# y split where it is made and loaded over h^T; wider weight ring in the RG phase; last block in written order

## The chip, the cores and the metric

One core of a Trainium2 chip runs the whole program. The metric is the device time of one execution in microseconds (us). Beside it stands the profiled execution, whose span runs from its first to its last instruction.

## What is computed

One layer of a hybrid mixer on 1024 latent tokens of width D = 2048, with 256 context tokens whose final states seed the latent scans. Cut to the latent path:

```python
hx = rmsnorm(x, norm_g) * (1 + sc_x) + sh_x           # shift, scale, gate: silu(c) @ w_mod
px = split(hx @ w_in)                                 # q k | v | o | z | gates | xr | zr
h  = mlstm_bidir(conv_silu(q, k), v, gates)           # 4 heads, column-major token order
ym = rmsnorm_per_head(h) * m_norm_g * sigmoid(o) * silu(z)
xl = dwconv(xr)                                       # RG-LRU: 1024 channels
r, i = sigmoid(w_r . xl + b_r), sigmoid(w_i . xl + b_i)   # block-diagonal, both directions
a  = exp(-8 * r * softplus(-lam))
hr = scan(a, sqrt(1 - a**2) * i * xl)                 # forward plus backward
yr = hr * silu(zr)
x  = x + gt_x * (concat([ym, yr]) @ w_out)
return rmsnorm(x, final_g)
```

## The kernel before

Every float32 product is made of three TensorE (PE) products of fp32r halves: a tile t is split into t_hi = fp32r(t), a copy on ScalarE (ACT), and t_lo = t - t_hi, a subtraction on VectorE (DVE), and hi.hi, hi.lo and lo.hi are summed in PSUM.

**h^T and y.** The normed input stands transposed in SBUF as 16 pairs hxh[j], hxl[j] of 128x1024. The output projection needs y in the same form, and y tile j takes the place of hxh[j], hxl[j], once the last unit that reads h^T is past it. A y tile is 128 channels x 1024 tokens. Two come from each of four heads, eight from the RG blocks (RG0 to RG7, 128 channels each). Fifteen go to a DRAM tensor yD, one DMA each on ACT's queue (L981 for the RG blocks, a like line at the end of each head); the last, RG7's, is split straight into hxh[15], hxl[15] (L978, L979).

**Weights.** Class Ring streams w_in and w_out: SyncE (SP) loads raws of 128x1024 (512 KB) into two buffers, each raw is cut into pieces of 128x512, split by ACT (whi, L228) and DVE (wlo, L229), in order, three pieces ahead at most. In the output phase three more pieces are added (ring.widen). A unit's 96 matmuls of w_in read four pieces (ct_unit, L1276, L1279, L1282), a block of the output 16 pieces, one for each j.

**The RG phase.** For each i there is a unit xr and a unit zr (sigmoid and product at L1459 and near it), and a generator x_rg that runs beside the units: convolution (POOL L740, three DVE steps L742), the split of the result xs/xl (ACT L1388, DVE L1389), eight gate tiles of three matmuls each (L1394 to L1396) into PSUM, sigmoids (ACT L935), the products i*x (POOL L937), exp and tanh (ACT L948, L949), sqrt (L952), then on DVE a sum and two products (L957, L958), the scan (L959), for both directions; POOL adds the two (L969), DVE multiplies by the gate (L973).

**The y stage.** From the last zr unit (zr7) on, y tiles are loaded in halves of 128x512 on GpSimd's (POOL) queue into two buffers (y_load, yst, L1422), and split over h^T by ACT (L1438) and DVE (L1439), 30 times: the half with tokens 0 to 511 ahead of out(0,0), two tiles for a hook at each j; the other half within the blocks that follow.

**The output phase.** out_unit(hf, db) makes 512 tokens x 512 columns: 16 j x 4 token tiles x 3 matmuls (L1475 to L1477) into one PSUM tile mm of two halves and two tiles mx. A hook of the next block evacuates it: times gt (DVE L1512), plus x from a tile xpc (POOL or DVE, L1513; one buffer), Square with its sum into fst (ACT L1514, which writes its square back to the PSUM tile), times final_g (L1515). After the fourth block of a token half, finish() takes the mean, square root and reciprocal (L1519 to L1521) and scales and stores (L1524 to L1527). The last block (1,3) has its weights in the place of y tiles of h^T, and goes token tile by token tile (L1563 to L1565).

**Order.** Units and generators are interleaved by a clock that the program runs when it is built; the instructions of each engine then stand in a fixed order that a list scheduler sets from priorities, and an engine works in that order. A DMA queue is the sequence of DMA starts on its engine; up to eight of POOL's are under way at a time.

Of the kernel before, what the change touches and what calls it, by code (L numbers as in the profile page):

```python
# [257 lines left out]
def tile_hymba(ctx: ExitStack, tc: tile.TileContext, x, x_t, ctx_t, vecs_t, w_mod_a, w_mod_g, b_mod, w_in,  # L258
# [21 lines left out]
    yD = dram.tile([16, 128, SEQ], F32, name="yD")  # L280
# [1135 lines left out]
    def y_load(hf, pool, bufs):

        done, ts = ysp[hf]
        while len(ts) < bufs and done + len(ts) < KT - 1 and ("y", KORD[done + len(ts)]) in xflag:
            j = done + len(ts)  # L1420
            t = pool.tile([128, 512], F32, tag="gw", bufs=bufs, name=f"yst{hf}_{j}")
            POOL.dma_start(out=t, in_=yD[KORD[j]][:, 512 * hf:512 * hf + 512])  # L1422
            ts.append(t)

    def y_split(n, hf, pool, bufs):

        for _ in range(n):
            j, ts = ysp[hf]
            if j >= KT - 1:
                clk.until(lambda: ("y", KORD[j]) in xflag)  # L1430
                return
            if not ts:
                clk.until(lambda: ("y", KORD[j]) in xflag)
                y_load(hf, pool, bufs)
            t = ts.pop(0)
            o = slice(512 * hf, 512 * hf + 512)
            with hp(tc, P['y']):
# [4 lines left out]

    for n, i in enumerate(RG_ORDER[1:]):
# [86 lines left out]
    for hf in range(2):  # L1530
        for db in range(4):
            if (hf, db) != (0, 0):
                todo = pend

                def hook(j):
                    if todo and j == 0:
                        vecs(*todo[0:2])
# [8 lines left out]
                    if hf and db == 0 and j == 0:
                        y_split(KT, 1, op, GWB)
                    if hf == 0 and db >= YD0 and j % 2 == 0 and j >= YJ0:
                        y_split(1, 1, op, GWB)

# [73 lines left out]
```

## Time and profile before

| | |
|---|---|
| median of three runs | 1891.2 us (1890.71 to 1900.89) |
| the profiled execution | 1890.24 us, span 1888.5 |
| PE busy | 1815.2 us, 96% |
| DVE, ACT, POOL busy | 896.5, 779.7, 284.5 us |
| mean granted PE clock | 0.99 |
| DMA | 224.5 MB, 119 GB/s |

Where PE's row is nearly full, the time is that of its matmuls and what breaks them. Two things break them: a wait for another engine's result, which the list of waits names, and a clock below 1.00 of 2.4 GHz, which stands in the windows. A window's count of matmuls holds both, so it is compared with the count of a stretch in which nothing happens.

### The profile page before, as it was taken

To read this page: it belongs to the slowest core of one execution; us is meant where nothing else is said; L and a number is where in the kernel's file an instruction comes from. 1 tells how busy PE (TensorE), PEld (TensorE's weight loads), DVE (VectorE), ACT (ScalarE), POOL (GpSimd) and SP (SyncE) were. 2 spreads that over 40 slices of the span, in tenths; PEclk is the share of its full clock that TensorE was granted. 3 is DMA by queue.
4 is the path that set the end of the run, shared out by engine and by line. 5 is a ranking of instruction groups with operands and counts; after the bars stand their busy time and mean duration, and the time that the engine had idled before them with its cause. 6 is when DMAs were issued, how large, how long until landed. Compare 5 with 4: busy or idle time off the path is not lost.

```text
span 1888.5 us, 24095 instructions
## 1 busy us (share of the span) xinstructions
PE 1815.2 (96%) x9114; PEld 1483.5 (79%) x9114; DVE 896.5 (47%) x1632; ACT 779.7 (41%) x1209; POOL 284.5 (15%) x382
## 2 busy tenths in 40 slices
PE   6998999999999999999999999999999989999996
PEld 2557999787897879887898877777888767888775
DVE  5576552446424654345425433564444555334422
ACT  5346542356445331233112333655555634233311
POOL 0000000012002200011001201232112323222220
PEclk9999999999999999999999999999999999999998
DMA  9975674223212433333332213112112345446523
GB/s 381 398 248 158 174 194 108 58 54 76 78 47 58 105 109 107 88 93 81 92 111 81 55 46 106 51 58 58 46 50 59 128 144 179 137 141 221 168 92 117
DMA packets 225365, 224.50 MB, mean 119 GB/s; under 512 B 25664, under 2 KB 184528, under 8 KB 225248
## 3 DMA queue, kind: packets, MB, share of 16 engines
q1 hardware_dynamic: 217200, 199.17, 35.1%
q10 hardware_dynamic: 5264, 14.88, 2.1%
q0 software_dynamic: 2784, 8.92, 1.4%
q8 instruction: 71, 1.16, 0.3%
q14 instruction: 46, 0.38, 0.1%
HBM read 202.92 MB, written 20.00 MB: 118 GB/s over the span
## 4 chain that ended last, share of the span: by engine, by line
PE 61%; DMA 12%; issue 11%; DVE 7%; ACT 6%; POOL 3%; SPq 0%; ACTq 0%; POOLq 0%; DVEq 0%
PE mm L1282 11%; PE mm L1276 11%; PE mm L1279 11%; DMA xpc<-in_x_dram 5%; PE mm L1319 2%; PE mm L1321 2%; PE mm L1322 2%; DMA yst<-yD 2%; POOL res L1513 2%; PE mm L627 2%; PE mx L505 1%; DMA r<-in_w_mod_g_dram 1%; PE mx L1207 1%; DMA wm<-in_w_mod_a_dram 1%; PE mx L1208 1%
## 5 line engine op out<-in xcount | busy, mean ns | idle before, releaser
L229 DVE TENSOR_TENSOR wlo<-raw,whi 128x512 fp32r<-128x512 f32 (+2 forms) x396 | 288.0, 736 | 574.5 <-ACT whi L228 568.3
L228 ACT ACTIVATE whi<-raw 128x512 fp32r<-128x512 f32 (+2 forms) x396 | 243.2, 624 | 561.5 <-PE mm L1279 247.2
L1276 PE MATMUL mm<-hxh,whi 128*128 128x512 f32 x1184 | 385.5, 406 | 0.3 <-DVE Gx L1308 0.3
L1282 PE MATMUL mm<-hxh,wlo 128*128 128x512 f32 x1184 | 375.1, 398 | 4.2 <-DVE wlo L229 4.2
L1279 PE MATMUL mm<-hxl,whi 128*128 128x512 f32 x1184 | 372.0, 395 | 0.0
L1282 PEld LDWEIGHTS mm<-hxh,wlo 128*128 128x128 f32 x1184 | 223.0, 189 | 57.9 <-DVE wlo L229 6.7
L1279 PEld LDWEIGHTS mm<-hxl,whi 128*128 128x128 f32 x1184 | 222.9, 188 | 52.9
L1276 PEld LDWEIGHTS mm<-hxh,whi 128*128 128x128 f32 x1184 | 221.5, 189 | 49.6 <-ACT s L1306 0.5
L1319 PE MATMUL mm<-whi,hxh 128*128 128x256 f32 x384 | 110.2, 287 | 0.3 <-DVE s L1357 0.2
L1321 PE MATMUL mm<-wlo,hxh 128*128 128x256 f32 x384 | 108.1, 281 | 0.0
L1322 PE MATMUL mm<-whi,hxl 128*128 128x256 f32 x384 | 107.4, 281 | 0.0
L1475 PE MATMUL mm<-whi,hxh 128*128 128x512 f32 x224 | 90.1, 402 | 6.3 <-ACT whi L228 6.1
L1476 PE MATMUL mm<-wlo,hxh 128*128 128x512 f32 x224 | 90.4, 404 | 3.3 <-DVE wlo L229 3.3
L1477 PE MATMUL mm<-whi,hxl 128*128 128x512 f32 x224 | 89.4, 399 | 0.0
L1476 PE MATMUL mx<-wlo,hxh 128*128 128x512 f32 x224 | 89.0, 397 | 0.0
L1475 PE MATMUL mx<-whi,hxh 128*128 128x512 f32 x224 | 89.0, 400 | 0.0
L1477 PE MATMUL mx<-whi,hxl 128*128 128x512 f32 x224 | 88.8, 396 | 0.0
L1033 DVE SCALAR_TENSOR_TENSOR r<-r,cols,r 128x256 f32<-128x256 f32 x120 | 60.5, 504 | 38.0 <-DMA r<-in_w_mod_g_dram 35.9
L1319 PEld LDWEIGHTS mm<-whi,hxh 128*128 128x128 f32 x384 | 72.4, 189 | 1.1 <-PE mx L1256 0.6
L1321 PEld LDWEIGHTS mm<-wlo,hxh 128*128 128x128 f32 x384 | 72.4, 188 | 0.3
L1322 PEld LDWEIGHTS mm<-whi,hxl 128*128 128x128 f32 x384 | 72.2, 189 | 0.0
L1179 ACT ACTIVATE D<-D,gxAC 128x128 f32<-128x128 f32 x64 | 25.5, 401 | 112.8 <-POOL D L1178 112.7
(324 smaller groups left out, 3086.5 us busy)
## 6 DMA issues: line engine op xcount, KB each, us to landing
raw<-in_w_in_dram SPq DMA_DIRECT2D x134, 512.0 KB
wm<-in_w_mod_a_dram SPq DMA_DIRECT2D x64, 512.0 KB
raw<-in_w_out_dram SPq DMA_DIRECT2D x64, 512.0 KB
r<-in_w_mod_g_dram SPq DMA_DIRECT2D x128, 128.0 KB
xT<-in_x_t_dram SPq DMA_DIRECT2D x16, 512.0 KB
NI<-niD SPq DMA_DIRECT2D x64, 128.0 KB
xpc<-in_x_dram SPq DMA_DIRECT2D x32, 256.0 KB
yD<-s ACTq DMA_DIRECT2D x15, 512.0 KB
```

What stands on the lines that cost most here:

```text
L228: self.nc.scalar.activation(out=hi, in_=src, func=AF.Copy)
L229: self.nc.vector.tensor_tensor(out=lo, in0=src, in1=hi.bitcast(F32), op=SUB)
L1033: DVE.scalar_tensor_tensor(out=a, in0=t, scalar=silc[:, k:k + 1], in1=a, op0=MUL, op1=ADD)
L1276: PE.matmul(out=ps[:, ts], lhsT=hi, rhs=hxh[k][:, ts], start=(k == 0), stop=False)
L1279: PE.matmul(out=ps[:, ts], lhsT=hi, rhs=hxl[k][:, ts], start=False, stop=False)
L1282: PE.matmul(out=ps[:, ts], lhsT=lo, rhs=hxh[k][:, ts], start=False, stop=(k == KT - 1))
L1319: PE.matmul(out=o, lhsT=hxh[k][:, sl], rhs=hi, start=(k == 0 and tt % 2 == 0), stop=False, skip_group_check=True)
L1321: PE.matmul(out=o, lhsT=hxh[k][:, sl], rhs=lo, start=False, stop=False, skip_group_check=True)
L1322: PE.matmul(out=o, lhsT=hxl[k][:, sl], rhs=hi, start=False, stop=(k == KT - 1), skip_group_check=True)
L1475: PE.matmul(out=pst[jt], lhsT=hxh[j][:, sl], rhs=hi, start=(j == 0), stop=False)
L1476: PE.matmul(out=pst[jt], lhsT=hxh[j][:, sl], rhs=lo, start=False, stop=False)
L1477: PE.matmul(out=pst[jt], lhsT=hxl[j][:, sl], rhs=hi, start=False, stop=(j == KT - 1))
```

## The change

- yD becomes two DRAM tensors. put_y splits each of the fifteen y tiles where it is made: an ACT copy of 128x1024 into a free tile (og in a head, the backward scan's tile in an RG block), a DVE subtraction of 128x1024 in place, a store of the hi part on ACT's queue and of the lo part on SP's.
- y_load and y_split go, and with them 30 ACT copies and 30 DVE subtractions of 128x512. y_fill loads hi and lo of a whole tile (128x1024, 512 KB) into hxh[j], hxl[j]: 30 loads, 15.7 MB where 7.9 MB were read, all on POOL's queue, from zr7's step 2 on, as its steps leave the tiles.
- ring.widen adds two pieces (whi and wlo) from the RG phase on; they go at j = 9 of out(0,0), before the output phase's three come.
- xpc has two buffers and is loaded two tiles ahead; the Square writes to an SBUF tile; the sum of three of the four parts of the mean is taken at db = 2, the square root takes the fourth.
- The last block keeps written order on PE, and each of its token tiles has a PSUM tile of its own to begin with: mx, mx, a half of mm, a half of another mm.

The diff, cut to its core:

```diff
-    yD = dram.tile([16, 128, SEQ], F32, name="yD")
+    yD = [dram.tile([16, 128, SEQ], F32, name=f"yD{u}") for u in range(2)]
...
-                ACT.dma_start(out=yD[8 + i], in_=y)
+                put_y(8 + i, y, it[1][:, 0:T])
...
+    def put_y(n, y, w):
+
+        act(out=w.bitcast(F32R), in_=y, func=AF.Copy)
+        DVE.tensor_tensor(out=y.bitcast(F32R), in0=y, in1=w, op=SUB)
+        ACT.dma_start(out=yD[0][n], in_=w)
+        SP.dma_start(out=yD[1][n], in_=y)
...
-            ACT.dma_start(out=yD[2 * h + v], in_=Y[v][:, 0:SEQ])
+            put_y(2 * h + v, Y[v][:, 0:SEQ], og[v][:, 0:SEQ])
+            yield 1.2
...
-            t = pool.tile([128, 512], F32, tag="gw", bufs=bufs, name=f"yst{hf}_{j}")
-            POOL.dma_start(out=t, in_=yD[KORD[j]][:, 512 * hf:512 * hf + 512])
...
-                act(out=hxh[j][:, o], in_=t, func=AF.Copy)
-                DVE.tensor_tensor(out=hxl[j][:, o], in0=t, in1=hxh[j][:, o].bitcast(F32), op=SUB)
...
+    def y_fill(k):
+
+        while y_n[0] <= min(k, KT - 2) and ("y", KORD[y_n[0]]) in xflag:
+            j = y_n[0]
+            POOL.dma_start(out=hxh[j], in_=yD[0][KORD[j]])
+            POOL.dma_start(out=hxl[j], in_=yD[1][KORD[j]])
+            y_n[0] += 1
+
+    def y_wait(j):
+        if j >= 9:
+            ring.x = None
+        clk.until(lambda: ("y", KORD[j]) in xflag)
+        y_fill(KT)
+
+    ring.widen(rg, 0, NXG, 1024, 512)
...
-        ps = ct_unit(("zr", i), (lambda k: y_load(0, rg, YB) if k < K0 else y_split(1, 0, rg, YB) if k < K1 else None) if last else None)
+        ps = ct_unit(("zr", i), (lambda k: y_fill(k - 2)) if last else None)
...
-    pst = out_unit(0, 0, lambda j: y_split(2, 0, rg, YB))
+    pst = out_unit(0, 0, y_wait)
...
-        t = op.tile([128, 512], F32, tag="xpc", bufs=1, name=f"xpc{tt}_{db}")
+        t = op.tile([128, 512], F32, tag="xpc", bufs=2, name=f"xpc{tt}_{db}")
...
-            act(out=ps, in_=r, func=AF.Square, accum_out=fst[tt][:, db:db + 1])
+            jk = op.tile([128, 512], F32, tag="jk", bufs=1, name=f"jk{tt}_{db}")
+            act(out=jk, in_=r, func=AF.Square, accum_out=fst[tt][:, db:db + 1])
...
+            if db == 2:
+                f = fst[tt]
+                DVE.tensor_reduce(out=f[:, 4:5], in_=f[:, 0:3], axis=AX.X, op=ADD)
+                DVE.tensor_scalar(out=f[:, 4:5], in0=f[:, 4:5], scalar1=1.0 / D, scalar2=EPS, op0=MUL, op1=ADD)
...
-        DVE.tensor_reduce(out=f[:, 4:5], in_=f[:, 0:4], axis=AX.X, op=ADD)
-        act(out=f[:, 5:6], in_=f[:, 4:5], func=AF.Sqrt, scale=1.0 / D, bias=eps)
+        act(out=f[:, 5:6], in_=f[:, 3:4], func=AF.Sqrt, scale=1.0 / D, bias=f[:, 4:5])
...
-    pst = out_tiles(3)
-    for jt in range(4):
+    pst = [mx_tile(), mx_tile(), mm_tile()[:, 0:512], None]
+    with in_order(tc, PE.engine):
+        for jt in range(4):
+            if jt == 3:
+                pst[3] = mm_tile()[:, 0:512]
```

Three places show what moved. In the rows a name's number is the buffer's own, `L...` the line of its kernel (most lines of the kernel after are 1 lower), and the words in brackets are the engines or DMA lanes whose results are waited for.

On POOL, at the last RG block: L937 (after: L936) are RG7's two products, L969 (L968) the sum of its scans. Before:

```order
L1422 DMA yst0_7_12427<-yD_72 128x512 [waits DMASW5_49,DVE_49]
L1422 DMA yst0_8_12516<-yD_72 128x512 [waits DMAHW3_49,DMASW6_49,DVE_49]
L1422 DMA yst0_9_12520<-yD_72 128x512 [waits DMASW7_49,DVE_49]
L1422 DMA yst0_10_12553<-yD_72 128x512 [waits DMASW0_49,DVE_49]
L937 TENSOR_TENSOR s_92_12464<-s_92_12464,s_88_12338 128x1024 [waits Activation_49]
L1422 DMA yst0_11_12557<-yD_72 128x512 [waits DMASW1_49,DVE_49]
L1422 DMA yst0_12_12584<-yD_72 128x512 [waits DMAHW4_49,DMASW2_49,DVE_49]
L1422 DMA yst0_13_12588<-yD_72 128x512 [waits DMAHW3_49,DMASW3_49,DVE_49]
L1422 DMA yst0_14_12615<-yD_72 128x512 [waits DMAHW2_49,DMASW4_49,DVE_49]
L937 TENSOR_TENSOR s_94_12534<-s_94_12534,s_88_12338 128x1024 [waits Activation_49]
L969 TENSOR_TENSOR s_92_12464<-s_92_12464,s_94_12534 128x1024 [waits DVE_49,Pool_49]
```

After:

```order
L1427 DMA hxl10_893<-yD1_73 128x1024 [waits DMASW5_49]
L1426 DMA hxh11_896<-yD0_72 128x1024 [waits DMASW6_49,PE_49]
L1427 DMA hxl11_901<-yD1_73 128x1024 [waits DMASW7_49]
L936 TENSOR_TENSOR s_92_12512<-s_92_12512,s_88_12390 128x1024 [waits DVE_49,Activation_49]
L1426 DMA hxh12_1007<-yD0_72 128x1024 [waits DMASW0_49,PE_49]
L1427 DMA hxl12_1012<-yD1_73 128x1024 [waits DMAHW2_49,DMASW1_49]
L1426 DMA hxh13_1015<-yD0_72 128x1024 [waits DMASW2_49,PE_49]
L1427 DMA hxl13_1020<-yD1_73 128x1024 [waits DMAHW2_49,DMASW3_49]
L1426 DMA hxh14_1120<-yD0_72 128x1024 [waits DMAHW1_49,DMASW4_49,PE_49]
L1427 DMA hxl14_1125<-yD1_73 128x1024 [waits DMAHW2_49,DMASW5_49]
L936 TENSOR_TENSOR s_94_12584<-s_94_12584,s_88_12390 128x1024 [waits Activation_49]
L968 TENSOR_TENSOR s_92_12512<-s_92_12512,s_94_12584 128x1024 [waits DVE_49,Pool_49]
```

Ahead of the rows of after stand 21 more loads. The first product had nine half-tile loads between it and the convolution and now has 24 loads of whole tiles ahead of it (one of them before the convolution); the second has four more half tiles before, six more whole ones after; each load waits for the lane of the load eight before it.

On PE, at RG0's gates, the first of the RG phase, which run beside the unit xr2 (pieces whi236 and on); mx299 to mx302 are the gates' PSUM tiles. Before:

```order
L1279 MATMUL mm305_10494<-hxl0_339,whi236_10400 128x512 x2
L1282 MATMUL mm305_10494<-hxh0_334,wlo236_10401 128x512 [waits DVE_49]
L1282 MATMUL mm305_10494<-hxh0_334,wlo236_10401 128x512
L1394 MATMUL mx299_10423<-s_7_10390,s_5_10340 128x512 [waits PE_49,Activation_49]
L1394 MATMUL mx300_10434<-s_7_10390,s_5_10340 128x512 [waits PE_49]
L1394 MATMUL mx301_10452<-s_7_10390,s_5_10340 128x512
L1394 MATMUL mx302_10463<-s_7_10390,s_5_10340 128x512 [waits PE_49]
L1276 MATMUL mm305_10494<-hxh1_342,whi236_10400 128x512
```

After:

```order
L1288 MATMUL mm305_10529<-hxh3_450,wlo236_10364 128x512 x2
L1282 MATMUL mm305_10529<-hxh4_545,whi237_10401 128x512 [waits Activation_49]
L1282 MATMUL mm305_10529<-hxh4_545,whi237_10401 128x512
L1285 MATMUL mm305_10529<-hxl4_550,whi237_10401 128x512
L1400 MATMUL mx299_10458<-s_7_10425,s_5_10375 128x512 [waits PE_49,Activation_49]
L1400 MATMUL mx300_10469<-s_7_10425,s_5_10375 128x512 [waits PE_49]
L1400 MATMUL mx301_10487<-s_7_10425,s_5_10375 128x512
L1400 MATMUL mx302_10498<-s_7_10425,s_5_10375 128x512 [waits PE_49]
```

The first gate matmul stood behind six matmuls of piece 236; now it stands behind all 24 of piece 236 and three of piece 237.

On ACT, between the sigmoids of the next block (L935, after L934): before, the store of y alone stood there (L981).

```order
L1388 ACTIVATE s_17_10605<-s_16_10560 128x1024 [waits DVE_49]
L935 ACT_TABLE_LOAD [waits PE_49]
L935 ACTIVATE s_19_10636<-mx308_10637,cols_102 128x512 [waits Pool_49]
L981 DMA yD_72<-s_10_10451 128x1024 [waits DVE_49]
L935 ACTIVATE s_19_10636<-mx309_10648,cols_102 128x512 [waits PE_49]
L935 ACTIVATE s_20_10659<-mx310_10660,cols_102 128x512 [waits PE_49]
L935 ACTIVATE s_20_10659<-mx311_10671,cols_102 128x512 [waits PE_49]
```

After:

```order
L934 ACT_TABLE_LOAD [waits PE_49]
L934 ACTIVATE s_19_10674<-mx308_10675,cols_103 128x512 [waits Pool_49]
L986 ACTIVATE s_12_10540<-s_10_10486 128x1024 [waits DVE_49]
L934 ACTIVATE s_19_10674<-mx309_10686,cols_103 128x512 [waits PE_49]
L988 DMA yD0_72<-s_12_10540 128x1024 [waits Activation_49]
L934 ACTIVATE s_20_10697<-mx310_10698,cols_103 128x512 [waits PE_49]
L934 ACTIVATE s_20_10697<-mx311_10709,cols_103 128x512 [waits PE_49]
```

The copy of put_y (L986) stands between the first and the second sigmoid, waits for DVE, and the store (L988) follows the second; six sigmoids of the block and the exp stand behind it.

## Rows read from the trace of the kernel before

**Rows 1.** The page, part 2: GB/s moved in 40 slices of 47.2 us.

```profile
GB/s 381 398 248 158 174 194 108 58 54 76 78 47 58 105 109 107 88 93 81 92 111 81 55 46 106 51 58 58 46 50 59 128 144 179 137 141 221 168 92 117
```

**Rows 2.** Waits of PE: line, for whom; us in total, times, longest us.

```profile
PE mm L1475 <- ACT whi L228: 6.1, 4, 2.5
...
PE mx L1394 <- ACT s L1388: 5.1, 3, 3.3
...
PE mm L1282 <- DVE wlo L229: 4.2, 2, 3.3
...
PE mm L1476 <- DVE wlo L229: 3.3, 6, 1.4
```

**Rows 3.** Windows: stretch, length, busy us (xcount) per engine, clock, DMA share, GB/s.

```profile
1166.00:1280.00 114.00, 103.92 (x425) 82.21 (x425) 66.87 (x54) 72.04 (x80) 31.20 (x16) 0.96 0.18 50
...
1300.00:1400.00 100.00, 100.00 (x430) 80.35 (x429) 46.79 (x42) 55.87 (x63) 20.99 (x13) 1.00 0.20 56
...
1465.00:1553.00 88.00, 79.40 (x315) 60.63 (x313) 50.22 (x59) 47.23 (x65) 26.00 (x27) 0.94 0.41 136
...
1553.00:1570.00 17.00, 14.83 (x61) 11.34 (x62) 11.59 (x15) 8.65 (x18) 10.32 (x11) 1.00 0.70 215
...
1600.00:1700.00 100.00, 100.00 (x433) 81.07 (x432) 39.70 (x53) 31.58 (x62) 28.10 (x21) 1.00 0.44 137
...
1710.00:1720.00 10.00, 10.00 (x45) 8.08 (x44) 4.08 (x8) 3.59 (x6) 0.00 (x0) 1.00 0.98 351
...
1750.00:1770.00 20.00, 18.41 (x72) 14.24 (x71) 7.04 (x10) 6.33 (x14) 3.88 (x3) 0.91 0.64 178
```

**Rows 4.** Timeline of the last block: start, us, instruction, idle before <- releaser.

```profile
1826.94 0.39 PE L1563 MATMUL mm<-hxh 128*128 128x512 f32 x1
...
1844.73 0.69 DVE L1513 TENSOR_TENSOR res<-res,xpc 128x512 f32<-128x512 f32 x1 [5.99 <-DMA xpc<-in_x_dram]
...
1846.23 0.79 PE L1563 MATMUL mm<-hxh 128*128 128x512 f32 x1 [5.73 <-ACT mm L1514]
...
1877.62 0.39 PE L1564 MATMUL mx<-hxl,hxh 128*128 128x512 f32 x1
...
1878.52 0.39 PE L1565 MATMUL mx<-hxh,hxl 128*128 128x512 f32 x1
...
1881.76 0.15 DVE L1519 TENSOR_REDUCE fs<-fs 128x1 f32<-128x4 f32 x1
```

**Rows 5.** Chain that ended last, 1465 to 1570: start, us, what.

```profile
1472.85 2.97 DMA yst<-yD
...
1477.50 2.89 DMA yst<-yD
...
1533.76 7.02 DMA yst<-yD
```

**Rows 6.** Waits of ACT, columns as for PE.

```profile
ACT hxh L1438 <- DMA yst<-yD: 28.6, 18, 5.1
```

**Rows 7.** Single lines L1388 and L973: ns min/median/max, first and last start.

```profile
L1388 ACT ACTIVATE s<-s x8: 1043/1058/1061, 1165.8 to 1478.7; 128x1024 fp32r<-128x1024 f32 x8
...
L973 DVE TENSOR_TENSOR s<-s,s x8: 1215/1226/1228, 1204.2 to 1528.2; 128x1024 f32<-128x1024 f32 x8
```

**Rows 8.** The same chain, RG7's last scan and POOL's sum.

```profile
1522.38 2.36 DVE s L959
...
1524.88 3.24 POOL s L969
```

**Rows 9.** Timeline from 1211.9 to 1212.4, columns as in the last block.

```profile
1211.91 2.41 POOL L937 TENSOR_TENSOR s<-s,s 128x1024 f32<-128x1024 f32 x1 [1.71 <-ACT s L935]
...
1212.38 2.48 DVE L229 TENSOR_TENSOR wlo<-raw,whi 128x512 fp32r<-128x512 f32 x1 [5.71 <-ACT whi L228]
```

**Rows 10.** Timeline near 1753, POOL's addition of x.

```profile
1753.39 1.29 POOL L1513 TENSOR_TENSOR res<-res,xpc 128x512 f32<-128x512 f32 x1 [2.01 <-DMA xpc<-in_x_dram]
```

**Rows 11.** DMA issues: form, KB each, median us from issue to landing.

```profile
yst<-yD POOLq DMA_DIRECT2D x30, 256.0 KB, 3.3
```

More of the change, by code (lines that the diff above doesn't have):

```diff
@@ L1411, in tile_hymba @@
     clk.spawn(x_rg(0, xp, zs[:, 0:SEQ]), 3.0, P['xrg'])
-    ysp = [[0, []], [0, []]]
     xflag["direct"] = True
[L1416 to L1420, printed above, removed]
-            t = pool.tile([128, 512], F32, tag="gw", bufs=bufs, name=f"yst{hf}_{j}")
-            POOL.dma_start(out=t, in_=yD[KORD[j]][:, 512 * hf:512 * hf + 512])
[L1423 to L1437, printed above, removed]
-                act(out=hxh[j][:, o], in_=t, func=AF.Copy)
-                DVE.tensor_tensor(out=hxl[j][:, o], in0=t, in1=hxh[j][:, o].bitcast(F32), op=SUB)
-            ysp[hf][0] += 1
-            y_load(hf, pool, bufs)
+    y_n = [0]
+    def y_fill(k):
[10 more added lines that the diff above has]
+    ring.widen(rg, 0, NXG, 1024, 512)
     for n, i in enumerate(RG_ORDER[1:]):
@@ L1537, in hook @@
                         vecs(*todo[0:2])
-                        xp_load(todo[0], todo[1], 0)
+                        for jt in range(2):
+                            xp_load(todo[0], todo[1], jt)
                     if todo and j in (1, 2, 3, 4):
@@ L1541, in hook @@
                         evac(todo[0], todo[1], jt, todo[2][jt], vec["gt"], vec["fg"], False)
-                        if jt < 3:
-                            xp_load(todo[0], todo[1], jt + 1)
+                        if jt < 2:
+                            xp_load(todo[0], todo[1], jt + 2)
                     if todo and todo[1] == 3 and 6 <= j < 10:
                         finish(4 * todo[0] + j - 6, True)
[L1546 to L1549, printed above, removed]
                 if (hf, db) == (1, 3):
@@ L1557, in tile_hymba @@
     hook(0)
-    pst = out_tiles(3)
-    for jt in range(4):
-        sl = slice((4 + jt) * 128, (5 + jt) * 128)
-        for j in range(KT):
-            hi, lo = hxh[j][:, 0:512], hxl[j][:, 0:512]
-            PE.matmul(out=pst[jt], lhsT=hxh[j][:, sl], rhs=hi, start=(j == 0), stop=False)
-            PE.matmul(out=pst[jt], lhsT=hxh[j][:, sl], rhs=lo, start=False, stop=False)
-            PE.matmul(out=pst[jt], lhsT=hxl[j][:, sl], rhs=hi, start=False, stop=(j == KT - 1))
-        if jt == 0:
-            for q in range(1, 5):
-                hook(q)
-            vecs(1, 3)
-            xp_load(1, 3, 0)
-        evac(1, 3, jt, pst[jt], vec["gt"], vec["fg"], True)
-        if jt < 3:
-            xp_load(1, 3, jt + 1)
-        finish(4 + jt, True)
+    pst = [mx_tile(), mx_tile(), mm_tile()[:, 0:512], None]
[3 more added lines that the diff above has]
+                pst[3] = mm_tile()[:, 0:512]
+            sl = slice((4 + jt) * 128, (5 + jt) * 128)
+            for j in range(KT):
+                hi, lo = hxh[j][:, 0:512], hxl[j][:, 0:512]
+                PE.matmul(out=pst[jt], lhsT=hxh[j][:, sl], rhs=hi, start=(j == 0), stop=False)
+                PE.matmul(out=pst[jt], lhsT=hxh[j][:, sl], rhs=lo, start=False, stop=False)
+                PE.matmul(out=pst[jt], lhsT=hxl[j][:, sl], rhs=hi, start=False, stop=(j == KT - 1))
+            if jt == 0:
+                for q in range(1, 5):
+                    hook(q)
+                vecs(1, 3)
+                for q in range(2):
+                    xp_load(1, 3, q)
+            evac(1, 3, jt, pst[jt], vec["gt"], vec["fg"], True)
+            if jt < 2:
+                xp_load(1, 3, jt + 2)
+            finish(4 + jt, True)
     opp.__exit__(None, None, None)
```

8 lines of the change are left out of this document (3 added, 5 removed).

## The prediction

> **What bounds the kernel now.** I read the page first: [rows 1] has the traffic in 40 slices of 47 us. The first two slices move 381 and 398 GB/s, later ones mostly 50 to 220: memory is not the limit after the first 100 us. TensorE (PE) is busy 96% of the span, so what can be won is the rest: stretches in which PE waits, or runs at a lower granted clock. The waits of PE [rows 2] name the lines. The windows [rows 3] say how much a stretch loses: where nothing disturbs, PE starts 430 matmuls of 512 columns in 100 us while it works on the w_in units (0.2325 us each) and 433 in the output phase (0.231). A stretch with fewer has lost the difference, whether as waiting or as clock.
>
> Four stretches matter here.
> - 1166 to 1280, the first four RG blocks: 425 matmuls in 114 us where 490 would fit, so about 65 x 0.2325 = 15 us lost, 9.3 of it in waits that [rows 2] list (5.1 for the xs split, 4.2 for a w_lo piece, the longest 3.3 in both) and most of the rest at a granted clock of 0.96.
> - 1465 to 1553, from zr7's first matmul to out(0,0)'s last. The program has 96 + 24 (RG7's gates) + 192 matmuls there: 120 x 0.2325 + 192 x 0.2305 = 72.2 us of work in 87.4 us, 15.2 lost, at a mean clock of 0.94. The 17 us behind it start 61 of 73 matmuls: some 2.5 more.
> - 1750 to 1770: 72 of 86.6 matmuls, 3.4 us, lost in a wait for w_hi and at a mean clock of 0.91.
> - The end: the last block starts at 1826.94 and its 192nd matmul at 1878.52 [rows 4]. At 0.225 (four matmuls in 0.90 us just before the end) to 0.231 it would start 43.0 to 44.1 us after the first: 7.5 to 8.6 us lost, of which one wait is 5.73.
>
> **The change part by part.** *The y stage.* Before, each half tile goes round a loop on three engines: load 2.97, ACT copy, DVE subtraction, and the next load at 1477.50, 4.65 us after the one at 1472.85 [rows 5]. ACT, whose order is fixed, stands 28.6 us before such copies [rows 6], and RG7's sigmoids, w_hi pieces and tables stand behind them. The change takes the 30 copies and 30 subtractions out and lets 30 loads of 512 KB land in h^T's tiles. All of the 17.7 us is open to it. What is late next is the load itself, and the order of POOL shows where: 24 loads stand ahead of RG7's first product (L936), six more ahead of the second, and eight are in flight at a time, so the second product waits until 22 have landed. Its DVE, POOL and ACT steps behind that take 1.2 + 0.7 + 2.36 + 3.24 + 1.2 + 1.8 = 10.5 us [rows 7, 8]; 0.7 is a w_lo piece of half the size, 1.8 the two halves of the last copy and subtraction.
> PE, undisturbed, wants the w_lo piece behind RG7's second scan input at 1465.3 + 27.9 + 12 x 2.77 = 1526.4, y tile 14 at 1532 and tile 15 at 1534.7. The queue comes to the loads at about 1472.5, as before. Until the second product 22 x 0.524 = 11.5 MB of y and about 3.5 MB of w_out must move, until tile 14 15.2 and 4.5 MB. The densest row is 351 GB/s (1710 to 1720, [rows 3]), the page's best slice 398. At 351 the second product ends at 1472.5 + 42.7 + 2.4 = 1517.6, y7 at 1528, tile 14 lands at 1528.6: both in time, by 4 to 7 us. At 300 tile 14 is 6 us late, at 265 some 15. So the loads need some 330 GB/s, which rows reach but with little to spare. I take 3.2 us of delay (a rate of about 315, short waits for pieces behind L957 included): **-14.5**, between -17.7 (no wait) and -3.
>
> A row shows VectorE and GpSimd in each other's way: a w_lo subtraction, half the size of the 1.23 one, took 2.48 while POOL worked on its product [rows 9]. The Trainium skill, "SBUF — State Buffer", section "SBUF: two separate sides", says the port pair of the two is an exclusive lock, and that a DMA issued from GpSimd can starve because its descriptors cannot be written meanwhile; the trace agrees on the lock, and no run here shows the starving. By that rule up to a DVE operation of 1.2 us would stand before each of 22 loads at its worst; with half of them hit for half of it the sum would lose 6.6 us, unless the eight in flight cover it.
>
> *The RG start.* Two more pieces of w_in let PE run further ahead: the order shows the first gates 21 matmuls later, the third ones 29 later, from the fourth on the same pattern. 21 matmuls are 4.9 us of work put before waits of 3.3 at most, so all 9.3 can go, and the clock behind them. Against it stands put_y: in RG0 to RG2 its ACT copy (1.06 [rows 7]) and its DVE subtraction (1.23) enter the chain, the copy between the sigmoids of the next block's gates where it waits for the y of the block before. I count three times 1.4 back. **-6**, between -10 and +4 (3 x 2.3 added, with a gain of 3). From RG3 on PE has no waits here, and 2.3 us of ACT and DVE work per block lie beside units of 22 us (96 matmuls): nothing.
>
> *The heads.* put_y adds 2 x (1.06 + 1.23) us per head, and an SP store ahead of later raw loads, which waits for the subtraction. PE's waits in the heads name none of these lines. **+1**, from 0 to +3.
>
> *Two x tiles (xpc).* POOL waited 2.01 us for the one buffer at 1753.39 [rows 10], ACT's square behind it, w_hi behind that. With a second buffer the load runs beside the evacuation of the tile before. **-3**, from 0 to -3.4. The square's write to SBUF instead of PSUM I cost at nothing: it is off PE's path.
>
> *The last block.* Its second tile shared a PSUM tile with the first, whose evacuation waited 5.99 us for x [rows 4]. Now it has its own and PE never returns. The lost 7.5 to 8.6 go; the reduction of 0.15 us and its hand-over leave the tail. **-8.3**, from -7 to -9.
>
> Sum: -14.5 - 6 + 1 - 3 - 8.3 = -30.8. The profiled execution took 1890.24 (span 1888.5), so 1859.4; the median of three runs is 1.0 higher: **1860**.
>
> **The rivals.** *(a) The loads set the pace.* At 265 GB/s, half way between the 215 of 1553 to 1570 [rows 3] and the 315 that I take, tile 14 comes 15 us late: the y stage gives -3 instead of -14.5, **1872**. For it: a pair of loads took 7.02 us beside other traffic [rows 5], 75 GB/s for the pair; against it: only two were in flight.
> A load on this queue into hxh also changes the type, which no load of before does. The Trainium skill, "DMA: Bandwidth & Descriptors", section "SWDGE vs HWDGE vs iDMA", says that a float32r destination always casts; it gives no rate, and no run here shows one.
> *(b) The RG start gives nothing*, because put_y's copy holds the sigmoids and the blocks are bound by their own chain: +6, **1866**.
> *(c) Slower: the loads go nearly one at a time.* The median from issue to landing is 3.3 us for 256 KB [rows 11]. If a load of 512 KB takes between 3.3 and 4 us and they do not overlap, the 30th lands at 1472.5 + 30 x 3.3 = 1571.5 to 1592.5, and RG7's second product waits for the 22nd. out(0,0) ends 5.5 us after that, at 1577 to 1598 where it was 1553: the y stage costs +24 to +45 instead of -14.5, **1899 to 1920**. It decides from 3.0 us per load. Against it: eight are allowed in flight and wait for nothing but the lane.
> The Trainium skill, "DMA: Bandwidth & Descriptors", section "Anatomy of one DMA — SWDGE (gpsimd) path", fits a DMA as 2.0 us and bytes at 436 GB/s, 3.2 us for 512 KB as an estimate; 256 KB would be 2.6 where the trace has 3.3, and by it the serial case would come to the lower end.
> *(d) The pieces do not help and the last block alone works:* DVE's w_lo pieces would stand behind RG7's scan steps (L957), which wait for POOL, and PE for them as before: -8.3 - 3 and little else, **1879**.
>
> **How the numbers follow.** Forecast 0.55 (1850 to 1865), (a) 0.18, (b) 0.12, (c) 0.06, (d) 0.05, and 0.04 for less than 1850. The range takes the forecast, (b) and (a) with its bounds: 1850 to 1875. A measurement of this kernel tells about 0.5% from no change, 9.5 us: below 1881.7 lie all but (c), so faster 0.92; (c) is split by 1900.7: same 0.03, slower 0.05.
>
> **What would show it.** In the trace after: PE from zr7's first matmul to out(0,0)'s last in 73 to 77 us; if L1469 waits for DMA of hxh or hxl tiles, it is (a) or (c), and the landing times (under 2 us apart, or 3) say which. PE's waits for xs splits near 1198 and 1231 gone; if instead sigmoids come late behind L986, it is (b). No wait in the last block and the last matmul 43 to 44 us after its first; no POOL wait for xpc of over 1 us. It is wrong if y's second half, stored on SP, holds raw loads so that PE waits for w_hi in the heads, or if RG7's second product stands behind loads past 1520.

## The result, and the profile after

The changed kernel took 1866.9 us (median of four, 1863.8 to 1870.6), 0.9868 of the kernel before (95% interval 0.982 to 0.9916); a second comparison (after_again) gave 1867.3 and 0.9853 (0.983 to 0.9875). The forecast was 1860, its range 1850 to 1875. The profiled execution took 1863.8 (span 1862.0) where the sum had 1859.4.

The page, PE's busy time (1815.2 before) and the traffic in 40 slices of 46.6 us; [rows 1] is the traffic before. The slices 32 and 33 (191 and 288 GB/s, before 128 and 144) are the y stage:

```profile
PE 1801.4 (97%) x9114; PEld 1478.5 (79%) x9114; DVE 898.1 (48%) x1625; ACT 772.2 (41%) x1190; POOL 284.8 (15%) x382
...
GB/s 383 398 261 149 172 201 112 68 48 73 57 98 56 106 101 131 73 78 106 101 132 84 61 45 137 28 91 67 64 71 71 191 288 155 135 125 238 168 120 119
```

PE's waits that answer to [rows 2] (line, for whom; us in total, times, longest). The waits for w_hi in the output phase are nearly gone (6.1 to 0.8), the one in the last block is gone; those for the xs split (L1394, before L1388) are not, and there are new ones for sigmoids (L934). The wait for w_lo beside the units (L1282 of [rows 2], 4.2) is gone:

```profile
PE mx L1400 <- ACT s L1394: 6.1, 3, 3.7
...
PE mm L1470 <- DVE wlo L228: 4.6, 5, 1.6
...
PE mx L1400 <- ACT s L934: 2.9, 2, 2.4
...
PE mm L1469 <- ACT whi L227: 0.8, 1, 0.8
```

Windows that answer to [rows 3] (stretch, length, busy us and count per engine, clock, DMA share, GB/s). The first holds the first four RG blocks: 441 matmuls where 425 were, but at a mean clock of 0.99 where it was 0.96. The second is zr7's first matmul to out(0,0)'s last: 75 us where 87.4 were, at a clock of 1.00 where it was 0.94. The next four show the loads, the last the place of the one x buffer (81 of 86.6 matmuls; 72 before):

```profile
1166.00:1280.00 114.00, 104.31 (x441) 82.56 (x441) 73.76 (x61) 69.95 (x81) 30.52 (x16) 0.99 0.21 65
...
1461.00:1536.00 75.00, 73.44 (x317) 59.13 (x316) 39.13 (x39) 36.08 (x44) 29.19 (x35) 1.00 0.84 290
...
1480.00:1490.00 10.00, 10.00 (x44) 8.08 (x44) 1.38 (x2) 5.02 (x7) 3.06 (x7) 1.00 1.12 407
...
1490.00:1500.00 10.00, 10.00 (x44) 8.07 (x43) 2.74 (x2) 8.89 (x10) 4.31 (x8) 1.00 1.12 407
...
1500.00:1510.00 10.00, 10.00 (x44) 8.09 (x43) 4.94 (x4) 8.28 (x10) 6.75 (x8) 1.00 1.16 412
...
1510.00:1520.00 10.00, 8.44 (x36) 6.43 (x35) 6.08 (x6) 1.15 (x2) 0.45 (x1) 1.00 0.92 324
...
1740.00:1760.00 20.00, 18.85 (x81) 14.80 (x80) 7.74 (x13) 7.68 (x14) 0.00 (x0) 1.00 0.41 131
```

The y loads of 512 KB, from the list of DMA issues (KB each, median us from issue to landing), which answer to [rows 11]:

```profile
hxl<-yD POOLq DMA_DIRECT2D x15, 512.0 KB, 11.3
...
hxh<-yD POOLq DMA_DIRECT2D x15, 512.0 KB, 11.1
```

The last block, as [rows 4] (start, us, instruction): 43.3 us from its first matmul to its last, 51.6 before, and a square root that no longer waits for a reduction after L1510:

```profile
1809.16 0.39 PE L1561 MATMUL mx<-hxh 128*128 128x512 f32 x1
...
1852.48 0.39 PE L1563 MATMUL mm<-hxh,hxl 128*128 128x512 f32 x1
...
1855.11 0.69 DVE L1510 TENSOR_TENSOR res<-res,fg 128x512 f32<-128x512 f32 x1 [0.79 <-ACT jk L1509]
...
1855.11 0.29 ACT L1518 ACTIVATE fs<-fs 128x1 f32<-128x1 f32 x1
```

For what follows the span is cut at marks that every kernel here has: the last transpose of the heads (L1256, after L1262), the first matmul of out(0,0), the matmul 288 later (half of block (0,1)), the first of the last block, the last matmul. Each mark is the start of a row in PE's timeline, and the six parts add up to the span.

| kernel | heads end | RG | y | middle | last block | tail | span |
|---|---|---|---|---|---|---|---|
| before | 1140.4 | 351.7 | 86.1 | 248.7 | 51.6 | 10.0 | 1888.5 |
| after | 1141.8 | 347.5 | 73.7 | 246.2 | 43.3 | 9.5 | 1862.0 |
| after_again | 1142.2 | 349.8 | 73.3 | 246.4 | 43.3 | 9.6 | 1864.6 |
| e1_no_widen | 1144.1 | 358.1 | 77.7 | 246.5 | 43.3 | 9.5 | 1879.3 |
| e2_last_only | 1140.9 | 350.8 | 86.6 | 248.6 | 43.3 | 10.0 | 1880.2 |
| e3_xpc1 | 1141.5 | 349.7 | 70.0 | 250.6 | 43.3 | 9.5 | 1864.6 |
| e4_rg_unsplit | 1144.4 | 346.3 | 73.0 | 245.6 | 43.3 | 9.6 | 1862.2 |
| e7_mul_dve | 1143.1 | 349.9 | 69.3 | 246.3 | 43.3 | 9.5 | 1861.5 |
| e9_nowiden_unsplit | 1144.9 | 354.0 | 78.0 | 246.6 | 43.3 | 9.5 | 1876.3 |
| e10_nxg1 | 1147.8 | 347.6 | 75.0 | 246.3 | 43.3 | 9.6 | 1869.6 |
| e11_all_mul_dve | 1141.5 | 348.9 | 69.4 | 246.0 | 43.3 | 9.6 | 1858.6 |
| e12_nowiden_actstore | 1145.1 | 357.1 | 78.0 | 246.3 | 43.3 | 9.5 | 1879.3 |
| e13_dve_actstore | 1149.6 | 346.6 | 69.3 | 249.2 | 43.3 | 9.5 | 1867.6 |

Kernels that are the same in a part show its spread: RG 347.5, 349.8, 349.7 and 349.9 (after, after_again, e3, and e7, which differs only at RG7), 349.2 on the mean; before and e2 351.7 and 350.8, 351.3 on the mean. The heads' end varies most, by 8 us among kernels with the same program there. What a part gains by 2 us or less is not told from one profile.

In the RG start a good part of the spread is the granted clock, which differs between profiles of the same program there. The stretch 1190 to 1290 (columns as above) in before, e2_last_only, after and after_again:

```profile
1190.00:1290.00 100.00, 90.83 (x370) 71.75 (x369) 60.01 (x48) 55.34 (x63) 27.60 (x14) 0.95 0.20 57
...
1190.00:1290.00 100.00, 89.74 (x375) 70.88 (x374) 61.49 (x51) 55.95 (x65) 26.47 (x14) 0.98 0.20 57
...
1190.00:1290.00 100.00, 90.31 (x377) 71.12 (x376) 65.21 (x54) 58.07 (x68) 26.90 (x14) 0.98 0.24 73
...
1190.00:1290.00 100.00, 90.55 (x368) 71.13 (x367) 64.88 (x54) 56.36 (x66) 26.35 (x14) 0.95 0.24 73
```

At like clock the kernels before and after start as many matmuls here: 370 and 368 at 0.95, 375 and 377 at 0.98.

### The profile page after: what moved, and what is told of

Read it like the earlier page. It is cut to its first block, busy times and chain, and to the rows that moved or that the text cites. A ratio compares the mean times of both kernels' runs of the same rounds, so it can differ in the third digit from the quotient of the medians.

```text
span 1862.0 us, 24089 instructions
## 1 busy us (share of the span) xinstructions
PE 1801.4 (97%) x9114; PEld 1478.5 (79%) x9114; DVE 898.1 (48%) x1625; ACT 772.2 (41%) x1190; POOL 284.8 (15%) x382
## 3 DMA queue, kind: packets, MB, share of 16 engines
q8 instruction: 71, 1.16, 0.2%
## 4 chain that ended last, share of the span: by engine, by line
PE 75%; DMA 9%; DVE 6%; issue 4%; ACT 4%; POOL 1%; SPq 0%; ACTq 0%; DVEq 0%; POOLq 0%
PE mm L1288 12%; PE mm L1285 12%; PE mm L1282 12%; PE mm L1325 2%; PE mm L1327 2%; PE mm L1328 2%; DMA wm<-in_w_mod_a_dram 2%; DMA raw<-in_w_out_dram 2%; PE mm L1470 2%; PE mx L1469 2%; PE mx L1471 2%; PE mx L1470 2%; PE mm L1471 2%; PE mm L1469 2%; DVE wlo L228 1%
## 5 line engine op out<-in xcount | busy, mean ns | idle before, releaser
L1282 PE MATMUL mm<-hxh,whi 128*128 128x512 f32 x1184 | 385.2, 406 | 0.3 <-DVE Gx L1314 0.3
L1282 PEld LDWEIGHTS mm<-hxh,whi 128*128 128x128 f32 x1184 | 221.2, 189 | 49.3 <-ACT s L1312 0.5
L1507 POOL TENSOR_TENSOR res<-res,xpc 128x512 f32<-128x512 f32 x28 | 39.7, 1438 | 211.4 <-DMA raw<-in_w_out_dram 131.8
```

The lines of the kernel that those rows point to most:

```text
L1282: PE.matmul(out=ps[:, ts], lhsT=hi, rhs=hxh[k][:, ts], start=(k == 0), stop=False)
```

## The experiments

Each is an edit of the changed kernel, but for e2. All times are medians beside the kernel before on the same chip. It took 1892.0, 1896.9 and 1893.5 us beside the three groups of runs, so between groups the ratios are compared.

**The second profile of the changed kernel (after_again)** gives the spread; no edit.

> The changed kernel once more, unaltered, beside the runs below on one chip. What it gives is the spread of a stage from run to run: from the heads' last transpose to out(0,0)'s first matmul 347.5 us in its first profile, 349.7 and 349.9 in two kernels that are the same up to there; expected 347 to 351, and 70 to 74 for the next 288 matmuls.

1867.3; the parts are as expected.

**The pieces left out (e1).**

```diff
-    ring.widen(rg, 0, NXG, 1024, 512)
```

> The changed kernel without the two extra weight pieces in the RG phase (three pieces, as before, until the output phase). Theory: the RG start (first four RG blocks) has its gain of some 5 us from these pieces alone, since they let PE run 21 to 29 matmuls on before the first gates; without them that stretch falls back by 5 us or more, because put_y stays, and out(0,0) loses up to 2 more: 1872 to 1874. Rival: the gain there is from put_y taking DMA or ACT work away, or from the run; then the time stays at 1867 plus or minus 2.

1880.3, 0.9939 (0.9922 to 0.9956): more than expected. RG takes 358.1, 9 us more than with the pieces and 6.9 more than before the change (means of the profiles above); the y stage loses 4. PE's waits from 1145 to 1310:

```profile
PE mm L1288 <- DVE wlo L228: 6.6, 2, 4.6
...
PE mx L1400 <- ACT s L1394: 6.3, 3, 3.7
```

The wait for w_lo, which is 4.2 in [rows 2], is 6.6, the one for xs 6.3. With the remainders not shown PE waits 13.9 us here and 9.7 with the pieces, so about 4 of the 9 are waits; in much of the rest PE has a lower clock (1190 to 1290: 0.93, and 0.95 to 0.98 with the pieces). So the pieces are worth 9 + 4 = 13 us of the 26, and a part of what they cover in RG is what the change itself puts there (e9 below).

**One extra piece instead of two (e10).**

```diff
-NXG = 2
+NXG = 1
```

> The changed kernel with one extra weight piece in the RG phase instead of two. Theory: each piece puts 24 matmuls, 5.6 us, of work ahead of a late gate, and the waits in the RG start are 3 to 4 us long, so the first piece gives the larger part: 1870 to 1873, against 1880 with none and 1866 with two. Rival: both are needed, since only two together carry the splits of one raw: 1876 to 1880.

1871.5, 0.9864 (0.9835 to 0.9894), no more of the kernel before than with two: no total shows a gain from the second piece. RG 347.6, as with two; the y stage 75.0, between 77.7 and 73.5, which is too little above 73.5 to be told from one profile. In the RG start the first piece gives it all: PE waits 9.0 us there (0.7 for the xs remainder not shown) where it waits 9.7 with two. The last row is a wait in out(0,0), 1.56 with two pieces:

```profile
PE mx L1400 <- ACT s L1394: 4.0, 2, 2.7
...
PE mx L1400 <- ACT s L934: 2.7, 2, 2.3
...
PE mm L1288 <- DVE wlo L228: 1.6, 1, 1.6
...
1518.14 0.79 PE L1470 MATMUL mm<-wlo,hxh 128*128 128x512 f32 x1 [3.83 <-DVE wlo L228]
```

**The RG blocks' y stored unsplit**, with the pieces (e4) and without (e9, which also leaves out ring.widen as e1 does).

```diff
-                put_y(8 + i, y, it[1][:, 0:T])
+                ACT.dma_start(out=yD[0][8 + i], in_=y)
+                SP.dma_start(out=yD[1][8 + i], in_=y)
```

> The changed kernel with put_y's ACT copy and DVE subtraction left out for the seven RG blocks (both stores are made of the unsplit y, so what is computed is not the reference). Theory of the prediction: the copy between the sigmoids costs about 1.4 us in each of three blocks, 4 us: 1863, and PE's waits for the xs split and for sigmoids between 1190 and 1290 shrink from 9 us to 5. Rival: the blocks are bound by their own chain and the copy lies beside it: 1867 plus or minus 1.5, the waits as large.

1864.4, 0.9849 (0.983 to 0.9869); the total is not told apart from the changed kernel's. RG is 346.3 against 349.2 on the mean, but 347.5 in the one profile of the changed kernel with the same clock (1190 to 1290: 383 matmuls at 0.98, 377 there). The waits (below, 1145 to 1300) went from 9.7 to 8.4 with the 0.7 for the xs remainder that is not shown, not to 5. So with the pieces the splits cost 1 to 1.5 us, not 4: the sigmoids' wait falls from 2.9 to 1.2, and the one for the xs split stays. Most of the waits are there without put_y's splits. (Lines are one higher in this kernel.)

```profile
PE mx L1401 <- ACT s L1395: 6.5, 3, 4.3
...
PE mx L1401 <- ACT s L934: 1.2, 1, 1.2
```

> The changed kernel without the two extra weight pieces, and with the splits of the seven RG blocks' y left out (both stores are made of the unsplit y, so what is computed is not the reference). Without the pieces alone the kernel took 1880.3, and its stretch from the first RG gates to zr7's end 7.5 us longer than in the kernel before. Theory: these 7.5 us are put_y's copies and subtractions, which the pieces hide; without the splits they go, 1873 to 1875. Rival: put_y costs nothing in either (as with the pieces, where leaving it out changed that stretch by 0.2), and the 7.5 come from another order or from the run: 1878 to 1881.

1877.2, 0.9892 (0.9859 to 0.9925). The 7.5 and the 0.2 in this expectation were read from marks by counted matmuls, of which the trace lacks some; by the marks of the table they are 6.9, and 1.2 to 3. RG falls from 358.1 to 354.0: by these two profiles the splits cost 4.1 without the pieces. 2.7 over the kernel before remain.

**The lo store on ACT's queue**, without the pieces (e12). SP stood long at that store (engine, line, for whom; us in total, times, longest) in e1 from 1150 to 1300, with raw loads behind it; the second row is e12 in the same window:

```profile
SPq L989 <- DVE s L987: 20.4, 5, 10.5
...
SPq L989 <- DVE s L987: 12.0, 2, 10.6
```

Two of the five waits, 12.0 us with the longest, belong to the last head's two tiles (n below 8), whose stores this edit leaves on SP. It takes away 8.4 us, not 20.4.

```diff
-    ring.widen(rg, 0, NXG, 1024, 512)
...
-        SP.dma_start(out=yD[1][n], in_=y)
+        (SP if n < 8 else ACT).dma_start(out=yD[1][n], in_=y)
```

> The changed kernel without the two extra pieces, with the RG blocks' second store (the lo part) on ACT's queue instead of SP's. Without the pieces the RG stage took 358.1 us, 7 more than in the kernel before; leaving out the splits took 4.1 of it away. Theory: part of the rest is SP, which stood 20.4 us at that store with raw loads behind it (longest 10.5); moved, RG falls to 354 to 356, the total to 1877. Rival: the raws come early enough anyway and the store's place does not matter: 357 to 359, 1880.

1882.1, 0.9931 (0.9904 to 0.9959); RG 357.1. The rival holds for the RG blocks' stores: these 8.4 us of SP's wait cost PE nothing that can be seen, and its waits are no shorter than in e1:

```profile
PE mx L1400 <- ACT s L1394: 7.8, 3, 3.7
...
PE mm L1288 <- DVE wlo L228: 7.0, 2, 5.0
```

What the remaining 2.7 us are is open. The splits are counted and the place of the RG blocks' stores is excluded; the heads' two stores on SP were not tried, and two profiles of one kernel differ by nearly as much in RG (347.5 and 349.8).

**The last block alone (e2)**, in the kernel before: its tiles and its order on PE as in the diff of the change, one x tile.

> The kernel before with the new last block alone (own PSUM tiles, written order); one x tile, old tail, old y stage. Theory: the wait of 5.7 us and the low clock behind it go: last block 43 to 44 us from first to last matmul, 8 us less: 1883. Rival: with one x tile the evacuations of the last block still come late, and the third and fourth tile or the tail wait instead: gain of 3 us or less, 1888 or more.

1882.8, 0.9952 (0.9935 to 0.997). The DVE addition still waits 5.37 us for its x, but nobody waits for it: 43.3 us from the first matmul to the last (start, us, instruction, idle before):

```profile
1826.89 0.39 PE L1566 MATMUL mx<-hxh 128*128 128x512 f32 x1
...
1844.05 0.69 DVE L1513 TENSOR_TENSOR res<-res,xpc 128x512 f32<-128x512 f32 x1 [5.37 <-DMA xpc<-in_x_dram]
...
1870.21 0.39 PE L1568 MATMUL mm<-hxh,hxl 128*128 128x512 f32 x1
```

**One x tile (e3).**

```diff
-        t = op.tile([128, 512], F32, tag="xpc", bufs=2, name=f"xpc{tt}_{db}")
+        t = op.tile([128, 512], F32, tag="xpc", bufs=1, name=f"xpc{tt}_{db}")
...
-                        for jt in range(2):
-                            xp_load(todo[0], todo[1], jt)
+                        xp_load(todo[0], todo[1], 0)
```

> The changed kernel with one x tile (xpc) instead of two. Theory: POOL and then ACT's square wait again for x in the middle blocks, w_hi behind that, and PE loses 2 to 3 us near 1740; the last block is not touched, since its tiles no longer share: 1868 to 1870. Rival: the wait there came from the y stage's timing and not from the one buffer: the same as with two, 1866 plus or minus 1.5.

1867.8, 0.985 (0.9818 to 0.9882): no difference in the total. The middle is 4.4 us longer, with a wait of 2.34 us near 1740. It is not shown to come from the one tile: the w_hi pieces behind it waited last for their raw (second row), and e13 below, with two x tiles, has a wait of 2.25 in the same place (third row) and a middle of 249.2, where e7, also with two, has 246.3:

```profile
1742.32 0.71 PE L1469 MATMUL mm<-whi,hxh 128*128 128x512 f32 x1 [2.34 <-ACT whi L227]
...
1741.11 2.19 ACT L227 ACTIVATE whi<-raw 128x512 fp32r<-128x512 f32 x4 [1.39 <-DMA raw<-in_w_out_dram]
...
1745.80 0.51 PE L1469 MATMUL mm<-whi,hxh 128*128 128x512 f32 x1 [2.25 <-ACT whi L227]
```

But the y stage is 3.5 us shorter. In the changed kernel POOL, with two x tiles at hand, does its products one right behind the other, and three w_lo subtractions on DVE take 5.12 us; PE waits 1.26 for one of them:

```profile
1542.53 2.97 POOL L1510 TENSOR_TENSOR res<-res,fg 128x512 f32<-128x512 f32 x2
...
1542.63 5.12 DVE L228 TENSOR_TENSOR wlo<-raw,whi 128x512 fp32r<-128x512 f32 x3 [2.46 <-ACT whi L227]
...
1544.41 0.50 PE L1470 MATMUL mm<-wlo,hxh 128*128 128x512 f32 x1 [1.26 <-DVE wlo L228]
```

With one x tile POOL pauses between its products, and three take 2.57:

```profile
1542.33 1.29 POOL L1510 TENSOR_TENSOR res<-res,fg 128x512 f32<-128x512 f32 x1 [0.83 <-ACT jk L1509]
...
1542.81 2.57 DVE L228 TENSOR_TENSOR wlo<-raw,whi 128x512 fp32r<-128x512 f32 x3 [1.53 <-ACT whi L227]
```

PE has no wait at all in block (0,1) there. So by these profiles the second tile costs some 3 us in block (0,1) and buys up to 4.4 in the middle; the totals show neither.

**RG7's products on DVE (e7)**, then those of all eight blocks (e11: the condition is `ini` alone), then those with the lo store on ACT's queue (e13: both edits).

```diff
-            POOL.tensor_tensor(out=it[d][:, 0:T], in0=it[d][:, 0:T], in1=xc, op=MUL)
+            (DVE if ini and i == RG_ORDER[-1] else POOL).tensor_tensor(out=it[d][:, 0:T], in0=it[d][:, 0:T], in1=xc, op=MUL)
```

> The changed kernel with RG7's two products i*x on DVE instead of POOL, so that they do not stand behind y's loads, nor run beside DVE. Theory: what is left of the loss in out(0,0) is a DVE product (L957) that takes 3.5 us instead of 1.2 because POOL's product runs at the same time, with a w_lo piece behind it; on DVE the wait of PE (1.56 us at 1512) goes: 1 to 2 us less, 1865 to 1866. Rival: the loads are what RG7's products and then PE wait for; then PE's waits for w_lo there stay and the time is the same or longer by DVE's 2.4 us.

1862.7, 0.9843 (0.9824 to 0.9862); the y stage 69.3 against 73.5. The place in the changed kernel (start, us, engine, line): the last sigmoid that POOL's second product reads ends at 1498.2, but the product stands behind loads, each of which waits for an earlier one to land, and starts at 1508.04, right behind the last. So it starts together with DVE's product L957; L957 takes 3.52, the w_lo piece comes behind it, and PE waits 1.56 for that piece:

```profile
1497.49 0.69 ACT L934 ACTIVATE s<-mx,cols 128x512 f32<-128x512 f32 x1
...
1507.48 0.54 POOL L1427 DMA_DIRECT2D hxl<-yD  x1 [0.53 <-DMA hxl<-yD]
...
1508.03 3.52 DVE L957 TENSOR_TENSOR s<-s,s 128x1024 f32<-128x1024 f32 x1
...
1508.04 2.42 POOL L936 TENSOR_TENSOR s<-s,s 128x1024 f32<-128x1024 f32 x1
...
1511.47 0.68 DVE L228 TENSOR_TENSOR wlo<-raw,whi 128x512 fp32r<-128x512 f32 x1
...
1512.20 0.50 PE L1470 MATMUL mm<-wlo,hxh 128*128 128x512 f32 x1 [1.56 <-DVE wlo L228]
```

With the product on DVE, L957 takes 1.22, and the wait is 0.47:

```profile
1511.75 1.22 DVE L957 TENSOR_TENSOR s<-s,s 128x1024 f32<-128x1024 f32 x1
...
1512.89 0.68 DVE L228 TENSOR_TENSOR wlo<-raw,whi 128x512 fp32r<-128x512 f32 x1
...
1517.60 0.51 PE L1470 MATMUL mm<-wlo,hxh 128*128 128x512 f32 x1 [0.47 <-DVE wlo L228]
```

The later waits, those of block (0,1), are gone as well, though POOL's products and the slow subtractions still stand there (5.14 us for three). The edit also changed DVE's order: RG7's second L957 runs at 1515.75, where in the changed kernel it ran at 1520.72 behind a late w_lo piece. So ACT, with w_hi pieces behind it in its order, stands 1.50 us for RG7's y tile instead of 7.64 (changed kernel, then this one):

```profile
1528.93 1.16 ACT L977 ACTIVATE hxh<-s 128x512 fp32r<-128x512 f32 x2 [7.64 <-DVE s L972]
...
1524.38 1.16 ACT L977 ACTIVATE hxh<-s 128x512 fp32r<-128x512 f32 x2 [1.50 <-DVE s L972]
```

That fits with pieces that are further ahead when PE comes to block (0,1), but is not shown to be the only cause. The theory holds for the wait at 1512, and the gain is larger than its 1 to 2 us. The rival is half right: no load held PE, but the loads held RG7's second product for 10 us and so put it beside L957. The edit takes the products out of the loads' queue and off POOL at once, so it does not part the two.

> The changed kernel with the products i*x of all eight latent RG blocks on DVE instead of POOL (RG7's alone there gave 1862.7). Theory: where POOL's product of 2.4 us runs, DVE's two-input operations beside it take 2.5 to 3.5 us instead of 0.7 to 1.2, so moving it costs DVE 1.2 and gives back 2: the RG start loses 1 to 3 us less, 1860 to 1862. Rival: DVE is full in that stretch (10.0 of 10 us in 1190 to 1200 and 1260 to 1280), and 2.5 us more per block make PE's waits longer: 1864 to 1868.

1863.5, 0.9824 (0.9796 to 0.9851). RG 348.9 is within the spread of 349.2, the y stage 69.4: what RG7's move gives, and nothing from the other seven that can be told.

> The changed kernel with all latent products i*x on DVE (as in the run before, 0.9824 of the kernel before) and the RG blocks' second store on ACT's queue. Theory: with the pieces SP stands 8.0 us at that store and PE's waits in the RG start are for xs splits and sigmoids, so the store's place gives 0 to 2 us there; the y stage keeps its 69.4 us: 0.980 to 0.983 of the kernel before, and 3 to 5 us under the changed kernel run beside it. Rival: the gain of the product's move was the run's: no difference beyond 2 us from the changed kernel.

1863.3, 0.9831 (0.9806 to 0.9856), beside the changed kernel's 1867.3 on the same chip; its own profile has a middle of 249.2. These three kernels have a y stage of 69.3 to 69.4 where the changed one has 73.3 and 73.7, and the lowest ratios of all; their intervals still overlap with the changed kernel's, so that they beat it is likely and not shown by the totals. The gain is that of the product's move; the store's place gives nothing that can be told.

## Why the prediction was right

The forecast time lay 7 us under the median and 4.4 under the profiled execution. Part of that nearness is luck: in the y stage a delay of the right size came from another place, and the RG start gave next to nothing. By its steps, with the spread of a part in mind:

- **The last block, -8.3.** Measured -8.3 from first to last matmul in every kernel with the new order, and -0.5 in the tail. Reason and size hold (e2).
- **The y stage, -14.5.** Measured -12.4 and -12.8 in the changed kernel. The reason for the gain holds: the loop of load, copy and subtraction is gone and the clock stays at 1.00. Between the marks PE waited 10.5 us before and 4.3 after, and much of the rest is clock. No run puts the old y stage beside the rest of the change, so its share rests on these marks and waits. What failed in the term is the load's rate. I took the densest row of the trace, 351 GB/s, as what the queues can do, and counted 3.2 us of delay at 315. That row is what was moved there, not what could be. The windows after show 407 to 412 GB/s from 1480 to 1510, eight loads of 512 KB in flight that land 11.1 us after their issue (378 GB/s), and the last load issued at 1507.5. It took 10.5 us, so it was there at 1518.0, some 10 us before PE wants tile 14 (1461.5 + 27.9 + 14 x 2.77 = 1528). In PE's list of waits no load stands. RG7's second product did stand behind the loads, as I had it (the last issue waits for the 22nd load), but until 1508.0 and not 1515. The delay that there is, of the size I had put in for the loads, comes by way of DVE: 1.56 us behind L957, which runs beside that product, and 2.8 in block (0,1) (e7, e3). So the term is nearly right for a wrong reason; the short waits behind L957 were named, but as the smaller part.
- **DVE and POOL in each other's way.** Rows show it again (3.52 us for a product of 1.2, 5.12 for three subtractions of 0.7). The Trainium skill, "SBUF — State Buffer", section "SBUF: two separate sides", has an exclusive lock between a DVE operation with two SBUF inputs and a GpSimd operation that reads SBUF, and a DMA from GpSimd that starves while DVE runs an operation in a two-port mode. The trace agrees on the first. The second is said of two-port modes and not of two inputs, so my estimate of 6.6 us carried it too far; the trace shows 407 to 412 GB/s beside DVE's two-input work. I had weighed the half that did not come, and not the half that did.
- **Rival (a) and (c), the loads.** Both fall with the rate: eight loads land in 11.1 us, 1.4 us each. The Trainium skill, "DMA: Bandwidth & Descriptors", section "SWDGE vs HWDGE vs iDMA", says that a float32r destination always casts, and gives no rate. These loads cast so, and the rows show no slowing by it.
- **The RG start, -6.** Measured -4.2 between the two first profiles, about -2 over all that are the same there (349.2 against 351.3), and nothing at like clock from 1190 to 1290. What failed is that all 9.3 us of waits can go. The w_lo waits went (4.2), but the xs split's are 6.1 where they were 5.1, and 2.9 for sigmoids are new: with the xs remainders 9.7 us where 10.1 were. My own sign, waits for xs splits gone, did not come. The pieces are worth 9 us (e1), but against a changed kernel without them, which is 6.9 slower here than the kernel before: put_y's splits are 4.1 of that (e9), where I had 4.2, and 2.7 are open. With the pieces the splits cost only 1 to 1.5 (e4). One piece would have done for RG (e10). Without any the y stage is 4 us longer (77.7 to 78.0 in e1, e9 and e12), a place that the prediction did not give to the pieces at all.
- **Rival (b)** is the nearest to what happened, in its time too (1866): RG gave a third of its term, or two thirds at best. Of its two reasons put_y's copy is the smaller. That the blocks are bound by their own chain fits with waits of 9.7 us after the change for xs splits and sigmoids, 8.4 without put_y's splits (e4); which step of the chain sets them no run takes apart.
- **Two x tiles, -3.** POOL no longer waits for x (26.1 us in 20 waits from 1560 on before, none after), and the middle gains 2.5, as predicted; but it is 249.2 in e13, which also has two tiles. What I had cost at nothing is POOL's faster pace: some 3 us in the y stage (e3). Net, the edit gives nothing that a total can show.
- **The heads, +1.** 1.4 and 1.8 in the two profiles; not settled, since the heads' end varies by 8 us between kernels that are the same there.

## What to carry to other kernels

The highest rate in a trace is only a bound from below on what the queues can do: look at what asked for the bytes there. A buffer that lets one engine run without pauses can slow a second one that works beside it; look for the second engine's operations that take longer than their median before the edit, and who stands behind them in its order. Where a widened buffer and new work come together, take the buffer away once: here it paid 13 us, of which about 4 went to cover work that came with it. And before a gain of a few us in a stage is put down to an edit, compare the granted clock there, and a second profile: here the same program had 368 or 377 matmuls in the same 100 us.

## What the runs showed of the hardware

- 30 loads of 512 KB on GpSimd's queue, eight in flight, ran at 407 to 412 GB/s with all other traffic, at a DMA share of 1.12 to 1.16; before, with two buffers, loads of 256 KB landed in 3.3 us in the median [rows 11] and the stretch moved 136 GB/s [rows 3]. The queue was not the limit there; whether it is the number in flight or the size that raised the rate, no run parts.
- A two-input DVE product of 128x1024 took 3.52 us with POOL's product beside it and 1.22 without; three subtractions of 128x512 took 5.12 us beside POOL's unbroken products and 2.57 where POOL paused between them.
- PE's mean granted clock was 0.94 in the 88 us from 1465 before, with the waits of [rows 2] in it, and 1.00 in the 75 us from 1461 after, with one wait of 1.56 in it. Before, it stood at 0.50 (1.2 GHz) in two places of that stretch, right behind waits of PE of 1.82 us (ended at 1498.7) and 2.52 (ended at 1516.0):

```profile
1499.50:1502.90 3.40, 3.40 (x9) 2.64 (x8) 2.56 (x4) 3.35 (x6) 1.09 (x2) 0.50 0.13 41
...
1516.60:1523.40 6.80, 5.39 (x13) 3.80 (x12) 6.80 (x7) 0.97 (x2) 0.00 (x0) 0.50 0.23 77
```
